# Where the matmul operands begin in a partition: moving the weight buffers and the operands that stream past them to 64 bytes past a multiple of 128

## The chip, the cores and the metric

One core of one Trainium2 chip runs the whole kernel in one launch. The metric is the device time of an execution in microseconds; lower is better. The notes below use the names of the profile: PE is TensorE's matmul, PEld its weight load, DVE is VectorE, ACT is ScalarE, POOL is GpSimd, SP issues most DMAs.

## What is computed

Two transformer blocks run one after the other on a sequence of 256 tokens with a model width of 1024. The first has a mixer of four kinds of linear attention, a cross attention to a memory of 256 rows, and a gated feed-forward part with a causal convolution of width 3. The second has two layers, each of three kinds of attention and another such feed-forward part:

```python
def reference(x, mem, positions, ...):
    x = first_block(x, mem, positions, ...)    # mixer, cross attention, conv FFN
    x = second_block(x, ...)                   # 2 x (three attentions, conv FFN)
    return x

# one feed-forward part, D_FF = 2816
    u = causal_dwconv(h @ w_up[l], conv_w[l], conv_b[l])
    gate, up = u[..., :D_FF], u[..., D_FF:]
    x = x + (jax.nn.silu(gate) * up) @ w_down[l]
```

Nearly all the arithmetic is products of an activation of 256 columns (the tokens) with weight matrices that are read once.

## The kernel before

Activations lie feature by feature: a partition holds a feature, and 256 columns of 4 bytes hold the tokens, so an operand of one product is 1024 bytes in a partition. Every number that enters a weight product is split into a high part that the fast 4-byte matmul type (float32r) holds and a low part, the rest. The weights come in 339 chunks of at most 1024 columns, in the order of use: SP loads a chunk into `raw`, ACT writes the high part `whi` and DVE the low part `wlo` (`load`, lines 396 to 414, three buffers of each). A product of 128x128 weights with 256 tokens is then three matmuls (`mm_f`, lines 422 to 431):

```python
            nc.tensor.matmul(ps, wh, xh[:, k, :], start=s, stop=False, skip_group_check=True)
            nc.tensor.matmul(ps, wh, xl[:, k, :], start=False, stop=False, skip_group_check=True)
            nc.tensor.matmul(ps, wl, xh[:, k, :], start=False, stop=e, skip_group_check=True)
```

The second argument is the stationary operand: PE loads its 128 columns. The third is the streaming operand, whose 256 columns pass through. So 128x128 weights are loaded for each matmul, and the load for the next one runs while the present one streams. In `mm_t` (lines 433 to 442), used where the result is wanted token by token, the roles are turned: the activation is stationary and the weights stream.

The stages, in order of time: the mixer (`block1_mix`, products into `psz`, `psq`, `psr`, `pst`), the keys of the memory (`psk`), the mixer's output product (`psW` from `oh`), the cross attention (`psv`, `psq`, and `po` from `xph`, whose stationary operand is the value tile `vh`), its output product (`psW` from `xoh`), and then three times a feed-forward part (`ffn`, tags f0, l0f, l1f) with a layer of attention (`attn`: `psp`, `pst`, then `psW` from `aoh`) before the second and third. A feed-forward part has 1056 matmuls up (`psU`, from `xh`, `xl`) and 528 down (`psD`, from `gh`, `gl`). A scheduler orders the instructions of each engine from the program's text and its own costs.

Tiles are given addresses by pools that stand one behind another in a partition, so an odd size moves all that follow. In `ffn` (line 627) a small tile `gpad` of 8, 16 or 72 columns (32, 64 or 288 bytes) is put ahead of `gh` and `gl`. By the built program's addresses the operands begin in a partition, in bytes past a multiple of 256:

| stationary in `mm_f` | streaming in `mm_f` | others |
|---|---|---|
| `whi`, `wlo` 128 | `xh`, `xl` 160; `gh`, `gl` 160 (f0), 192 (l0f), 160 (l1f); `mh`, `ml`, `oh`, `ol` 224; `xoh`, `xol` 0; `aoh`, `aol`, `lath` 128 | `xph` 64 streams past `vh` 224; `kh` 0 past `qh` 0 |

Blocks of 128 weights begin at multiples of 512 bytes in their buffer, and the blocks of an activation at multiples of 1024, so these differences hold for nearly all products. (Exceptions are the weights of `t0`, 280 and 264 columns wide, and four blocks behind them.)

Two masks of 128x128, `triu` and `strict`, are loaded with the constants of block 1 into `cst1` (line 747). Lines 912 and 913 copy them on DVE into the last 256 columns of `levr`, whose first 896 a DMA on POOL's queue fills (line 750).

## Time and profile before

| | us |
|---|---|
| median of three runs | 1169.15 (1167.93 to 1175.37) |
| the profiled execution, as timed | 1173.19 |
| its span in the profile | 1171.4 |

The profile shows one execution. Busy times of PE are sums of intervals in which a matmul was under way. Matmuls are pipelined: one lasts about 0.28 us in the trace while the next starts some 0.115 us after it. What counts is therefore the number of matmuls in a stretch. A row for a stretch counts each instruction that was under way in it, so two of the matmuls it counts began before it.

### The profile page before, as it was taken

The numbers are of one execution on the slowest core, as the hardware profiler recorded it, in microseconds if no ns is written. First come the engines' busy times: TensorE is split into PE (matmuls) and PEld (weight loads), VectorE is DVE, ScalarE is ACT, GpSimd is POOL, SyncE is SP. The second block draws the span as 40 slices with busy tenths as digits, with TensorE's granted clock in tenths as the row PEclk, the third lists the DMA queues.
The fourth block names the chain that finished last, engine by engine and source line by source line (L and its number), as shares of the span: only waits on it lengthen the run. The fifth ranks groups of instructions, "written<-read, shape, count | busy, mean of one in ns | idle before, by whom it ended". The sixth has DMA issues, their size and how long they took to land.

```text
span 1171.4 us, 23197 instructions
## 1 busy us (share of the span) xinstructions
PE 1141.4 (97%) x9148; PEld 1098.4 (94%) x9148; DVE 937.7 (80%) x1887; ACT 668.4 (57%) x1178; POOL 109.0 (9%) x137
## 2 busy tenths in 40 slices
PE   8999999999999999998999999999999999999996
PEld 7799888989999999997989999999998999999996
DVE  7887869586599997568997899986577978999854
ACT  6562545566476566553555676664545556766642
POOL 5500201010010000222000200001120002000000
PEclk9999999999999999998999999999999999999999
DMA  7522242556455655553423555556543235556552
GB/s 244 167 76 77 69 144 73 178 175 218 129 167 195 197 183 193 185 165 121 142 95 110 179 193 186 191 188 197 184 143 124 93 125 171 189 187 194 184 192 87
DMA packets 51948, 184.68 MB, mean 158 GB/s; under 512 B 5888, under 2 KB 6784, under 8 KB 51584
## 3 DMA queue, kind: packets, MB, share of 16 engines
q1 hardware_dynamic: 51408, 182.23, 48.1%
q8 instruction: 71, 1.16, 0.4%
q0 software_dynamic: 144, 0.46, 0.1%
q10 hardware_dynamic: 288, 0.52, 0.1%
q14 instruction: 37, 0.30, 0.1%
HBM read 182.14 MB, written 1.05 MB: 156 GB/s over the span
## 4 chain that ended last, share of the span: by engine, by line
PE 87%; DVE 9%; ACT 2%; issue 1%; DMA 0%; SPq 0%; POOL 0%; DVEq 0%; ACTq 0%
PE psU L431 10%; PE psU L429 10%; PE psU L430 10%; PE psD L429 5%; PE psD L431 5%; PE psD L430 5%; PE psp L429 3%; PE psp L430 3%; PE po L451 3%; PE psp L431 3%; PE psW L429 3%; PE psW L431 3%; PE psW L430 2%; DVE wlo L411 2%; PE pss L451 2%; PE pst L442 2%
## 5 line engine op out<-in xcount | busy, mean ns | idle before, releaser
L410 ACT ACTIVATE whi<-raw 128x1024 fp32r<-128x1024 f32 (+5 forms) x411 | 362.9, 898 | 311.8 <-PE psU L430 60.0
L411 DVE TENSOR_TENSOR wlo<-raw,whi 128x1024 fp32r<-128x1024 f32 (+5 forms) x411 | 423.9, 1043 | 135.6 <-ACT whi L410 133.1
L429 PE MATMUL psU<-xh,whi 128*128 128x256 f32 x1056 | 295.9, 280 | 0.0
L431 PE MATMUL psU<-xh,wlo 128*128 128x256 f32 x1056 | 295.4, 280 | 0.2 <-DVE wlo L411 0.2
L430 PE MATMUL psU<-xl,whi 128*128 128x256 f32 x1056 | 295.2, 280 | 0.0
L431 PEld LDWEIGHTS psU<-xh,wlo 128*128 128x128 f32 x1056 | 198.8, 188 | 0.4 <-DVE wlo L411 0.4
L429 PEld LDWEIGHTS psU<-xh,whi 128*128 128x128 f32 x1056 | 198.9, 188 | 0.1
L430 PEld LDWEIGHTS psU<-xl,whi 128*128 128x128 f32 x1056 | 198.8, 188 | 0.1
L429 PE MATMUL psD<-gh,whi 128*128 128x256 f32 x528 | 147.1, 279 | 0.0
L431 PE MATMUL psD<-gh,wlo 128*128 128x256 f32 x528 | 147.1, 279 | 0.0
L430 PE MATMUL psD<-gl,whi 128*128 128x256 f32 x528 | 147.1, 279 | 0.0
L534 POOL TENSOR_TENSOR ssa<-ssa,ssq 128x256 f32<-128x256 f32 x61 | 55.4, 912 | 721.3 <-ACT ssq L532 442.2
L666 DVE SCALAR_TENSOR_TENSOR y<-zb,prm,y 128x256 f32<-128x256 f32 x264 | 114.3, 482 | 0.0
L430 PEld LDWEIGHTS psD<-gl,whi 128*128 128x128 f32 x528 | 99.3, 188 | 0.0
L429 PEld LDWEIGHTS psD<-gh,whi 128*128 128x128 f32 x528 | 99.3, 188 | 0.0
L431 PEld LDWEIGHTS psD<-gh,wlo 128*128 128x128 f32 x528 | 99.3, 188 | 0.0
L429 PE MATMUL psp<-xh,whi 128*128 128x256 f32 (+1 forms) x288 | 85.4, 297 | 0.0
L430 PE MATMUL psp<-xl,whi 128*128 128x256 f32 (+1 forms) x288 | 84.3, 293 | 0.0
L431 PE MATMUL psp<-xh,wlo 128*128 128x256 f32 (+1 forms) x288 | 84.0, 292 | 0.0
L657 ACT ACTIVATE y<-zb,prm 128x256 f32<-128x256 f32 x132 | 67.2, 558 | 4.8 <-DVE zb L653 4.7
L442 PE MATMUL pst<-wlo,xh 128*128 128x256 f32 (+3 forms) x176 | 56.5, 321 | 1.9 <-DVE wlo L411 1.9
L429 PEld LDWEIGHTS psp<-xh,whi 128*128 128x128 f32 (+1 forms) x288 | 55.5, 193 | 3.0 <-issue 2.3
(456 smaller groups left out, 2350.2 us busy)
## 6 DMA issues: line engine op xcount, KB each, us to landing
raw<-in_wst_dram SPq DMA_DIRECT2D x319, 512.0 KB, 3.5
raw<-in_wst_dram SPq DMA_DIRECT2D x5, 448.0 KB, 3.3
cst<-in_c_dram SPq DMA_DIRECT2D x1, 1664.0 KB, 7.1
raw<-in_wst_dram SPq DMA_DIRECT2D x3, 396.0 KB, 2.9
mem<-in_memT_dram SPq DMA_DIRECT2D x1, 1024.0 KB, 5.3
raw<-in_wst_dram SPq DMA_DIRECT2D x2, 480.0 KB, 3.9
raw<-in_wst_dram SPq DMA_DIRECT2D x2, 420.0 KB, 7.2
raw<-in_wst_dram SPq DMA_DIRECT2D x2, 384.0 KB, 4.3
```

The source lines that it names most:

```text
L410: nc.scalar.activation(hi[:, a:b], raw[:, a:b], AF.Copy)
L411: nc.vector.tensor_sub(lo[:, a:b], raw[:, a:b], hi[:, a:b].bitcast(F32))
L429: nc.tensor.matmul(ps, wh, xh[:, k, :], start=s, stop=False, skip_group_check=True)
L430: nc.tensor.matmul(ps, wh, xl[:, k, :], start=False, stop=False, skip_group_check=True)
L431: nc.tensor.matmul(ps, wl, xh[:, k, :], start=False, stop=e, skip_group_check=True)
L442: nc.tensor.matmul(pss[t], xh[:, k, a], wl, start=False, stop=i == n - 1, skip_group_check=True)
L451: self.nc.tensor.matmul(out, lhsT, rhs, start=start, stop=stop, skip_group_check=True)
L534: (eng or nc.gpsimd).tensor_add(acc, acc, sq)
L657: nc.scalar.activation(y[:, e, u, :], z[:, e, 2:], AF.Identity, scale=fc[:, c + 2:c + 3], **kw)
L666: nc.vector.scalar_tensor_tensor(y[:, e, u, :], zs[u][:, e, j:j + T], fc[:, c + j:c + j + 1], y[:, e, u, :], ALU.mult, ALU.add)
```

## The change

Pads of 64 to 224 bytes are put ahead of the weight buffers and of five other groups of tiles, and `gh` and `gl` become slices of larger tiles. The two masks leave `cst1`; the DMA on POOL's queue brings them into `levr` together with the rest, and the later steps read them there. No product, load or conversion is added or taken away but the two copies of lines 912 and 913.

```diff
-GPAD = {"f0": 8, "l0f": 16, "l1f": 72}
+PAD = {"w": 16, "x": 56, "m": 16, "xo": 24, "lat": 8}
+GPAD = {"f0": 76, "l0f": 72, "l1f": 68}
...
+    def pad(self, pool, key):
+        if PAD[key]:
+            pool.tile([P, PAD[key]], F32, name="pad" + key)
...
             self.wraw = en("wraw", NRAW)
+            self.pad(en("wpad"), "w")
             self.whi = en("whi", NW)
...
+            self.pad(self.one, "x")
             self.prm1 = self.one.tile([P, _PWID1], F32, name="prm1")
...
-            big.tile([P, GPAD[tag]], F32, name="gpad")
-            gh = big.tile([P, NFF, T], F32R, name="gh")
-            gl = big.tile([P, NFF, T], F32R, name="gl")
+            gh, gl = (big.tile([P, NFF * T + P], F32R, name=n)[:, GPAD[tag]:GPAD[tag] + NFF * T].rearrange("p (k t) -> p k t", t=T)
+                      for n in ("gh", "gl"))
...
-                nc.gpsimd.dma_start(self.levr[:, 0:896], self.ap["c1"][:, _C1O["lev"][0]:])
+                nc.gpsimd.dma_start(self.levr, self.ap["c1"][:, _C1O["lev"][0]:])
...
-        tri, strict = self.c1("triu"), self.c1("strict")
         lev = self.levr
-        nc.vector.tensor_copy(lev[:, 896:1024], tri)
-        nc.vector.tensor_copy(lev[:, 1024:1152], strict)
+        tri, strict = lev[:, 896:1024].bitcast(F32), lev[:, 1024:1152].bitcast(F32)
...
+        self.pad(self.memp, "m")
         self.mh = self.memp.tile([P, KD, T], F32R, name="mh")
...
+        self.pad(m, "xo")
         oh = m.tile([P, KD, T], F32R, name="xoh")
...
+        self.pad(m, "lat")
         lh = m.tile([P, 3, T], F32R, name="lath")
```

By the built program's addresses the operands now begin as follows, and the last column is the start of the streaming operand less that of the stationary one, in bytes modulo 256, before and after (for `gh` modulo 128 the starts are 80, 64 and 48):

| products | streaming, after | stationary, after | difference before, after |
|---|---|---|---|
| `psU`, `psp`, `psz`, `psr`, `psq` <- `xh`, `xl` | 192 | 192 | 32, 0 |
| `psD` <- `gh`, `gl` in f0 | 208 | 192 | 32, 16 |
| the same in l0f | 192 | 192 | 64, 0 |
| the same in l1f | 176 | 192 | 32, 240 |
| `psW` <- `aoh`; `lath`; `kh` past `qh` | 192 | 192 | 0, 0 |
| `psW` <- `xoh` | 192 | 192 | 128, 0 |
| `psk` <- `mh`; `psW` <- `oh` | 64 | 192 | 96, 128 |
| `po` <- `xph` past `vh` | 0 | 64 | 96, 192 |
| `pst` <- `whi` past `xh` (`mm_t`) | 192 | 192 | 224, 0 |
| `psv` <- `whi` past `mh` (`mm_t`) | 192 | 64 | 160, 128 |

The order of the instructions changes only in the mixer: of some 8660 on PE about thirty lines of difference, none behind the first 350, and none of the products of the feed-forward parts. On DVE it changes around the two copies, at the end of the mixer's convolution. There DVE had, in the kernel before (`wlo` are weight conversions, `y` the convolution, `gl_p` gates):

```order
L411 TENSOR_TENSOR wlo<-raw,whi 128x512
L755 TENSOR_TENSOR z<-psz,iy 128x256
L411 TENSOR_TENSOR wlo<-raw,whi 128x512
L912 CAST levr<-cst_141 128x128
L411 TENSOR_TENSOR wlo<-raw,whi 128x512
L759 SCALAR_TENSOR_TENSOR y<-z,prm_86,y 128x256
L411 TENSOR_TENSOR wlo<-raw,whi 128x512
L759 SCALAR_TENSOR_TENSOR y<-z,prm_86,y 128x256
L859 TENSOR_SCALAR gl_p<-sm 128x8
L860 TENSOR_TENSOR gl_p<-sm,prm_86 128x8
L759 SCALAR_TENSOR_TENSOR y<-z,prm_86,y 128x256
L913 CAST levr<-cst_141 128x128
```

In the changed kernel the same place reads:

```order
L415 TENSOR_TENSOR wlo<-raw,whi 128x512
L764 SCALAR_TENSOR_TENSOR y<-z,prm_91,y 128x256
L415 TENSOR_TENSOR wlo<-raw,whi 128x512
L760 TENSOR_TENSOR z<-psz,iy 128x256
L415 TENSOR_TENSOR wlo<-raw,whi 128x512 x2
L764 SCALAR_TENSOR_TENSOR y<-z,prm_91,y 128x256
L864 TENSOR_SCALAR gl_p<-sm 128x8
L865 TENSOR_TENSOR gl_p<-sm,prm_91 128x8
L764 SCALAR_TENSOR_TENSOR y<-z,prm_91,y 128x256 x2
```

The two casts are gone, and one `z` stands a step or two later among the same conversions. On POOL's queue the place of the mask's DMA and of its readers is the same; before they were these rows:

```order
L750 DMA levr<-in_c_dram 128x896
L848 TENSOR_TENSOR sinR<-sinR,iy 128x256
L849 TENSOR_TENSOR cosR<-cosR,iy 128x256
L923 TENSOR_TENSOR G_659<-cst_141,glo 128x512
L923 TENSOR_TENSOR G_663<-cst_141,glo 128x512
```

and now they are these:

```order
L755 DMA levr<-in_c_dram 128x1152
L853 TENSOR_TENSOR sinR<-sinR,iy 128x256
L854 TENSOR_TENSOR cosR<-cosR,iy 128x256
L926 TENSOR_TENSOR G_662<-levr,glo 128x512
L926 TENSOR_TENSOR G_666<-levr,glo 128x512
```

The DMA has 256 columns more, and the products `G` read the mask from the tile that it fills.

## Rows read from the trace of the kernel before

**Rows 1.** The page: the span, busy time, clock, chain that ended last.
```profile
span 1171.4 us, 23197 instructions
...
PE 1141.4 (97%) x9148; PEld 1098.4 (94%) x9148; DVE 937.7 (80%) x1887; ACT 668.4 (57%) x1178; POOL 109.0 (9%) x137
...
PEclk9999999999999999998999999999999999999999
...
PE 87%; DVE 9%; ACT 2%; issue 1%; DMA 0%; SPq 0%; POOL 0%; DVEq 0%; ACTq 0%
```
**Rows 2.** Busy time by stretch: part of the mixer, the second block's attentions.
```profile
core 0: us, PE busy (x) PEld busy (x) DVE busy (x) ACT busy (x) POOL busy (x), PEclk, DMA share, GB/s
30.00:170.00 140.00, 135.15 (x940) 121.44 (x939) 111.86 (x278) 69.10 (x147) 24.47 (x30) 0.99 0.34 104
...
511.00:655.00 144.00, 138.78 (x1097) 130.03 (x1096) 118.93 (x340) 75.56 (x167) 11.94 (x11) 0.96 0.38 122
837.00:976.00 139.00, 135.78 (x1085) 127.80 (x1084) 111.03 (x325) 72.65 (x161) 11.50 (x11) 0.98 0.40 127
```
**Rows 3.** The same view: 100 us of psU in f0, l0f, l1f.
```profile
340.00:440.00 100.00, 100.00 (x859) 100.00 (x859) 96.34 (x154) 65.33 (x95) 0.00 (x0) 1.00 0.58 188
665.00:765.00 100.00, 100.00 (x858) 99.95 (x857) 94.69 (x150) 67.77 (x94) 0.00 (x0) 1.00 0.59 192
990.00:1090.00 100.00, 100.00 (x859) 100.00 (x859) 95.42 (x151) 66.94 (x93) 0.00 (x0) 1.00 0.58 189
```
**Rows 4.** The same view: 56 us of psD in f0, l0f, l1f.
```profile
452.00:508.00 56.00, 56.00 (x482) 56.00 (x482) 34.14 (x40) 31.61 (x44) 11.52 (x12) 1.00 0.58 189
780.00:836.00 56.00, 56.00 (x497) 56.00 (x496) 35.53 (x41) 29.63 (x40) 7.00 (x6) 1.00 0.59 195
1104.00:1160.00 56.00, 56.00 (x482) 56.00 (x481) 29.74 (x36) 26.68 (x36) 0.00 (x0) 1.00 0.49 157
```
**Rows 5.** The same view: unbroken psW from aoh, first and second layer.
```profile
641.24:649.15 7.91, 7.91 (x68) 7.91 (x67) 4.25 (x5) 2.74 (x4) 0.00 (x0) 1.00 0.41 140
962.94:971.09 8.15, 8.15 (x70) 8.15 (x69) 3.74 (x5) 2.50 (x3) 0.00 (x0) 1.00 0.41 145
```
**Rows 6.** The same view: psk and psW from oh; psW from xoh; pst of 256.
```profile
208.00:237.00 29.00, 29.00 (x244) 29.00 (x243) 14.92 (x24) 14.14 (x28) 0.00 (x0) 1.00 0.55 178
307.00:320.00 13.00, 13.00 (x112) 13.00 (x111) 5.76 (x9) 5.30 (x9) 0.00 (x0) 1.00 0.52 166
...
170.63:176.19 5.56, 5.56 (x49) 5.55 (x48) 2.59 (x4) 3.30 (x8) 0.00 (x0) 1.00 0.54 189
```
**Rows 7.** PE in order of time: first and last of ten consecutive matmuls into po.
```profile
281.10 0.28 PE L451 MATMUL po<-xpl,vh 128*128 128x256 f32 x1
...
282.18 0.28 PE L451 MATMUL po<-xpl,vh 128*128 128x256 f32 x1
```
**Rows 8.** Costliest groups of the page: counts of psU, psD, psp (one line of three).
```profile
L429 PE MATMUL psU<-xh,whi 128*128 128x256 f32 x1056 | 295.9, 280 | 0.0
...
L429 PE MATMUL psD<-gh,whi 128*128 128x256 f32 x528 | 147.1, 279 | 0.0
...
L429 PE MATMUL psp<-xh,whi 128*128 128x256 f32 (+1 forms) x288 | 85.4, 297 | 0.0
```
**Rows 9.** Tile levr and line 923: duration min/median/max in ns, first and last start.
```profile
L750 POOL DMA_DIRECT2D levr<-in_c_dram x1: 772/772/772, 39.3 to 39.3; - x1
L912 DVE CAST levr<-cst x1: 295/295/295, 39.8 to 39.8; 128x128 fp32r<-128x128 f32 x1
L913 DVE CAST levr<-cst x1: 219/219/219, 42.5 to 42.5; 128x128 fp32r<-128x128 f32 x1
...
DMA to landing us min/median/max: 6.4/6.4/6.4
...
L923 DVE TENSOR_TENSOR G<-cst,ghi x2: 684/684/685, 51.0 to 51.6; 128x512 fp32r<-128x512 f32 x2
```

More of the change, by code (lines that the diff above doesn't have):

```diff
@@ L211, in const_arrays @@
     c1["hind"] = hi2
-    c1["triu"] = (i[:, None] <= i[None, :])
-    c1["strict"] = (i[:, None] > i[None, :])
     lg = np.log(f(1) - np.exp2(f(-5) - np.arange(4, dtype=f))).astype(np.float64)
@@ L236, in const_arrays @@
     c1["decay"] = dec.reshape(P, -1)
-    c1["lev"] = np.concatenate(lev, 1)
+    c1["lev"] = np.concatenate(lev + [i[:, None] <= i[None, :], i[:, None] > i[None, :]], 1)
     c2["ident"] = np.eye(P)
@@ L707, in block1_mix @@
         self.cst1 = cp.tile([P, n2], F32, name="cst1")
-        n1 = _C1O["triu"][0]
+        n1 = _C1O["mlev"][0]
         m = self.mp = en("mix")
```

## The prediction

> **What bounds the kernel now.** I read the page first, then busy time by stretch, then PE in order of time. The page says that TensorE is the bound: PE is busy for 97% of the span and 87% of the chain that ended last is PE's, at a granted clock of 0.9 or more in all slices but one [rows 1]. So the next question is how fast PE's stream runs where nothing holds it up. In the feed-forward parts a row shows PE busy for all of its 100 us, DVE for 95 to 96, and 858 or 859 matmuls at a granted clock of 1.00, which is 2.4 GHz [rows 3]. Two of those began before the stretch, so a matmul starts every 100 / 857 = 116.7 ns.
>
> Here is what the reader should see next: the same form of matmul (128x128 weights, 256 columns, float32r), at the same clock, with PE busy throughout, has not one interval but several. I set each beside the difference d, the start of the streaming operand less that of the stationary one, modulo 256 bytes, from the addresses in the section on the kernel:
>
> - d = 32: psD in f0 and l1f, 56 / 480 = 116.7 ns [rows 4]; psU also 116.7 [rows 3].
> - d = 64: psD in l0f, 56 / 495 = 113.1 ns [rows 4]. Same code, same weights' order, only the operand's start differs.
> - d = 0: psW from aoh, 7.91 / 66 and 8.15 / 68 = 119.9 ns [rows 5].
> - d = 96: psk and psW from oh, 29 / 242 = 119.8 ns [rows 6].
> - d = 128: psW from xoh, 13 / 110 = 118.2 ns; d = 224: pst of 256 columns, 5.56 / 47 = 118.3 ns [rows 6].
>
> **Is it the difference, or the streaming start alone?** That decides the sign, because the change moves both operands. One place tells. In the cross attention xph streams from 64 (modulo 128) past vh, which starts at 96 there (d = 96). If a streaming start of 64 were what makes psD in l0f fast, these would take 113 ns. Nine intervals take 282.18 - 281.10 = 1.08 us, 120 ns each [rows 7], as the other pair with d = 96 does, with operands at 96 and 0 [rows 6]. So two pairs that differ in both starts but not in d agree, and two pairs with the same streaming start (64) and different d are 7 ns apart. I take it that the load of the next weights and the stream of the present matmul get into each other's way, and that how much depends on d.
>
> The Trainium skill speaks against this: "SBUF — State Buffer", section "SBUF: two separate sides", says that on the engines' side only the port pair shared by VectorE and GpSimd causes contention, and PE never waits on anyone. By it no start would matter and the change would cost nothing, near 1169 us. This trace disagrees with it by 7 ns a matmul between rows 4 and 5; I keep it as a rival.
>
> **The change part by part.** Nothing that PE does is added or removed; only d changes, so each term is matmuls times the step in their interval, from the d that they have to the d that they get.
>
> - psU, 3 x 1056 matmuls [rows 8], d from 32 to 0: 3168 x (119.9 - 116.7 = 3.2 ns) = 10.1 us. All on the path, PE being busy throughout [rows 3].
> - psD in l0f, 528 matmuls (a third of 3 x 528 [rows 8]), d from 64 to 0: 528 x (119.9 - 113.1 = 6.8) = 3.6 us.
> - psD in f0, 528, d from 32 to 16. No row has 16. It lies between 0 (+3.2) and 32 (nothing); I take the middle, 1.6 x 528 = 0.8 us. The far ends are 113.1 and 119.9: -1.9 to +1.7 us.
> - psD in l1f, 528, d from 32 to 240. Its neighbours are 224 (118.3) and 0 (119.9); middle 119.1, 2.4 x 528 = 1.3 us, with the same ends, -1.9 to +1.7 us.
> - psp, 3 x 288 [rows 8], of which 60 stream from lath at d = 0 before and after: 804 x 3.2 = 2.6 us. In the attention stretches PE is busy for 138.8 of 144 and 135.8 of 139 us [rows 2], but part of that is matmuls that wait for each other's results; I count four fifths, 2.1 us.
> - psz, psq and psr from xh: 144 + 288 + 96 = 528 by the loops, x 3.2 = 1.7 us; four fifths again (PE 135 of 140 us in the mixer [rows 2]), 1.4 us.
> - mm_t with 256 columns, 240 by the loops, d from 224 to 0: 1.6 x 240 = 0.4 us. The 144 with 264 or 280 columns have mixed starts before and after: nothing. With 512 columns (240) both operands change to d = 0 or 128 from 224 or 160; no row bounds it closely, I take nothing, with 240 x twice 1.6 = 0.8 us either way.
> - psk and psW from oh, 384, d from 96 to 128: -1.6 x 384 = -0.6 us. psW from xoh, 192, d from 128 to 0: 1.7 x 192 = +0.3 us. psW from aoh, 384, keeps d = 0: nothing. po from xph, 96, goes to d = 192, which no row has: between 113.1 and 120, -0.7 to 0; I take nothing.
> - The masks. Two copies of 0.295 and 0.219 us leave DVE [rows 9]. They stood in the mixer, where DVE is busy for 112 of 140 us and PE for 135 [rows 2], so PE's work hides them: nothing, with 0.5 us as the bound of the gain. The DMA on POOL's queue grows from 896 to 1152 columns. It was issued at 39.3 and landed 6.4 us later, near 45.7; the products G that now wait for it started at 51.0 [rows 9]. Stretched by 1152 / 896 it lands 8.2 us after its issue, at 47.5. That leaves 3.5 us, so nothing; if that cover were gone, DVE would stand in G with its weight conversions behind it, and PE's products of the mixer would come later by the same time, 3 us at worst.
>
> The sum is 10.1 + 3.6 + 0.8 + 1.3 + 2.1 + 1.4 + 0.4 - 0.6 + 0.3 = 19.4 us. The profiled execution took 1173.2 us (1171.4 of it span) and would take 1192.6. It stands 4 us above the median of 1169.15, which lies within the spread of the three runs, so on the median the same sum gives 1188.5 us, 1.7% slower. No other engine takes over: DVE had 4 to 5% to spare in psU [rows 3] and gets more when PE slows.
>
> **The rivals.**
> First, the streaming start alone decides, and 64 is the good one. Then psU, psp and the mixer's products go to 113.1: -3.6 x (3168 + 0.8 x 1332) = -15.2 us; aoh from 119.9, 384 x -6.8 = -2.6; psk, oh, -6.7 x 384 = -2.6; xoh, -5.1 x 192 = -1.0; f0 and l1f, at 80 and 48, between -3.8 and 0, say -1.9. That is -23.3 us, 1146. For it speaks psD in l0f, the only stream from 64 past weights at 0; against it the 120 ns of po [rows 7]. It decides from the point where a pair at 64 and 64 runs below 116.7. In that case DVE, at 95 to 96 of 100 us in psU [rows 3], would come within 2% of being the bound.
>
> Second, no start matters by itself or by d; the intervals come from something that the stages differ in, and the new kernel takes 1169 us. This is what the skill's rule above would make of it. Against it stand the three psD stretches, alike in all else and 3.6 ns apart.
>
> Third, slower by more: the writes of whi and wlo at the new start get slower too. DVE has 100 x 119.9 / 116.7 - 95.5 = 7 us of 103 to spare in psU, so it would have to lose more than 7% to be felt. Nothing in the trace shows this; with 10% psU would be 2 to 3 us longer in each 100, some 10 us over the three parts, 1199.
>
> **How the numbers follow.** Forecast 0.76; streaming start alone 0.13; no effect 0.08; still slower 0.03. The forecast's own range is 1181 to 1194: the sum less the fifths, the unknown d at their good ends and the mixer's terms (about 7 us), or with all of them at the bad end (about 4). The range of 8 in 10 leaves the first rival out and reaches down to the second: 1168 to 1195. About 1% (12 us) is what a measurement of this kernel can tell from no change. Slower by more than that is the forecast, but for the part where it comes out small, and the third rival: 0.76. Within 1%: 0.11. Faster: 0.13.
>
> **What would show it.** In the changed kernel 100 us of psU should hold about 836 matmuls (100 / 0.1199, and two) where 859 were; 56 us of psD in l0f about 469 where 497 were, and now fewer than in f0; psW from oh slightly more than before, psW from aoh the same. The mixer's end should move by 1 to 2 us at most. It is wrong if psU holds more than 870, and the rule on d falls if psD in l0f keeps its 497.

## The result and the profile after

The changed kernel takes 1187.56 us, the median of 4 executions (1183.63 to 1193.86); the kernel before, beside it on the same chip, 1169.37. The ratio is 1.0145, 95% interval 1.0113 to 1.0177: slower by 18.2 us, where 19.4 were forecast. (Ratios leave out executions more than 1.5% above the fastest of their kernel; in runs 6 and 9 below these belong to what is measured, and there I list all times as well.)

The page of the profiled execution, which took 1193.86 us, the longest of the four, has these lines in answer to [rows 1, 8]:

```profile
span 1192.1 us, 23193 instructions
...
PE 1164.1 (98%) x9148; PEld 1121.2 (94%) x9148; DVE 939.2 (79%) x1885; ACT 668.0 (56%) x1178; POOL 110.8 (9%) x137
...
PEclk9899989999999999998999999999999999999999
...
PE 89%; DVE 7%; ACT 2%; issue 1%; DMA 0%; SPq 0%; POOL 0%; DVEq 0%
...
L433 PE MATMUL psU<-xh,whi 128*128 128x256 f32 x1056 | 299.4, 284 | 0.0
...
L433 PE MATMUL psD<-gh,whi 128*128 128x256 f32 x528 | 148.2, 281 | 0.0
...
L433 PE MATMUL psp<-xh,whi 128*128 128x256 f32 (+1 forms) x288 | 86.1, 299 | 0.0
```

PE has as many instructions as before and 22.7 us more busy time; its share of the chain that ended last went from 87 to 89%. Next, busy time by stretch: 100 us of psU in f0, l0f and l1f, then 56 us of psD in each, which answer to [rows 3, 4]; then psW from aoh twice, psk with psW from oh, psW from xoh, and pst of 256 columns, which answer to [rows 5, 6].

```profile
core 0: us, PE busy (x) PEld busy (x) DVE busy (x) ACT busy (x) POOL busy (x), PEclk, DMA share, GB/s
350.00:450.00 100.00, 100.00 (x836) 100.00 (x835) 94.29 (x148) 62.76 (x92) 0.00 (x0) 1.00 0.56 185
680.00:780.00 100.00, 100.00 (x836) 100.00 (x835) 92.41 (x146) 65.27 (x90) 0.00 (x0) 1.00 0.56 185
1010.00:1110.00 100.00, 100.00 (x836) 100.00 (x835) 93.11 (x147) 65.53 (x92) 0.00 (x0) 1.00 0.56 184
461.00:517.00 56.00, 56.00 (x474) 56.00 (x474) 33.35 (x40) 31.59 (x44) 11.51 (x12) 1.00 0.58 183
792.00:848.00 56.00, 56.00 (x469) 56.00 (x468) 33.66 (x42) 29.16 (x39) 5.60 (x5) 1.00 0.54 183
1123.00:1179.00 56.00, 56.00 (x480) 56.00 (x480) 31.17 (x39) 27.34 (x37) 0.00 (x0) 1.00 0.49 160
...
650.50:658.41 7.91, 7.91 (x68) 7.91 (x67) 4.25 (x5) 2.75 (x4) 0.00 (x0) 1.00 0.44 141
979.98:988.12 8.14, 8.14 (x70) 8.14 (x69) 3.74 (x5) 2.50 (x3) 0.00 (x0) 1.00 0.45 148
214.00:243.00 29.00, 29.00 (x247) 29.00 (x246) 15.16 (x25) 14.23 (x28) 0.00 (x0) 1.00 0.54 178
312.00:325.00 13.00, 13.00 (x111) 13.00 (x110) 5.87 (x9) 5.21 (x9) 0.00 (x0) 1.00 0.48 163
176.65:182.21 5.56, 5.56 (x48) 5.56 (x47) 2.59 (x4) 3.28 (x7) 0.00 (x0) 1.00 0.57 189
```

Read with the count less two, as in the prediction: psU went from 116.7 to 100 / 834 = 119.9 ns, with 836 matmuls where 836 were forecast. psD in l0f fell from 497 matmuls to 469, to 119.9 ns, and is now the slowest of the three psD and no longer the fastest. psW from aoh, whose difference of starts d is 0 in both kernels, holds its 68 and 70. psk and psW from oh gained three matmuls (d from 96 to 128), psW from xoh lost one (d from 128 to 0), pst of 256 columns lost one (d from 224 to 0). The clock was 1.00 in all of these.

The stages start as follows (psk is the keys of the memory); a stage's gain is the change in the distance between starts. The columns "second" are a second profiled execution of the same changed kernel, taken later (run 10). The last column is the prediction's sum, each term put where its matmuls run: of psz, psq and psr 336 of 528 stand ahead of psk and 192 in the cross attention, and of the mm_t products with 256 columns most stand in the attention.

| stage | before, us | after | gain | after, second | gain | forecast |
|---|---|---|---|---|---|---|
| start to first psk | 178.9 | 185.0 | +6.1 | 178.2 | -0.7 | +0.9 |
| to first psU | 145.5 | 145.5 | 0 | 145.5 | 0 | +0.2 |
| psU, three together | 374.7 | 384.9 | +10.2 | 384.8 | +10.1 | +10.1 |
| psD f0 | 61.6 | 62.7 | +1.1 | 62.7 | +1.1 | +0.8 |
| psD l0f | 59.8 | 63.3 | +3.5 | 63.4 | +3.6 | +3.6 |
| psD l1f | 61.5 | 61.8 | +0.3 | 61.7 | +0.2 | +1.3 |
| attention, two layers | 279.1 | 278.6 | -0.5 | 278.6 | -0.5 | +2.4 |

### The profile page after: what moved, and what is told of

The parts are those of the page before. It is cut to its first block, busy times and chain, and to the rows that moved or that the text cites. A ratio compares the mean times of both kernels' runs of the same rounds, so it can differ in the third digit from the quotient of the medians.

```text
span 1192.1 us, 23193 instructions
## 1 busy us (share of the span) xinstructions
PE 1164.1 (98%) x9148; PEld 1121.2 (94%) x9148; DVE 939.2 (79%) x1885; ACT 668.0 (56%) x1178; POOL 110.8 (9%) x137
## 4 chain that ended last, share of the span: by engine, by line
PE 89%; DVE 7%; ACT 2%; issue 1%; DMA 0%; SPq 0%; POOL 0%; DVEq 0%
PE psU L435 10%; PE psU L434 10%; PE psU L433 10%; PE psD L435 5%; PE psD L433 5%; PE psD L434 5%; PE psp L433 3%; PE psp L434 3%; PE po L455 3%; PE psp L435 3%; PE psW L433 3%; PE psW L435 2%; PE psW L434 2%; PE pss L455 2%; DVE wlo L415 2%; PE pst L444 2%
## 5 line engine op out<-in xcount | busy, mean ns | idle before, releaser
L415 DVE TENSOR_TENSOR wlo<-raw,whi 128x1024 fp32r<-128x1024 f32 (+5 forms) x411 | 424.0, 1043 | 147.6 <-ACT whi L414 143.7
L433 PE MATMUL psU<-xh,whi 128*128 128x256 f32 x1056 | 299.4, 284 | 0.0
L435 PE MATMUL psU<-xh,wlo 128*128 128x256 f32 x1056 | 298.9, 283 | 0.1
L434 PE MATMUL psU<-xl,whi 128*128 128x256 f32 x1056 | 298.8, 283 | 0.0
L435 PEld LDWEIGHTS psU<-xh,wlo 128*128 128x128 f32 x1056 | 202.7, 192 | 0.3 <-DVE wlo L415 0.3
L434 PEld LDWEIGHTS psU<-xl,whi 128*128 128x128 f32 x1056 | 202.7, 192 | 0.1
L433 PEld LDWEIGHTS psU<-xh,whi 128*128 128x128 f32 x1056 | 202.7, 192 | 0.1
L444 PE MATMUL pst<-whi,xh 128*128 128x256 f32 (+3 forms) x176 | 57.2, 325 | 0.7 <-DVE z L760 0.7
```

The costliest lines, as they stand in the source:

```text
L415: nc.vector.tensor_sub(lo[:, a:b], raw[:, a:b], hi[:, a:b].bitcast(F32))
L444: nc.tensor.matmul(pss[t], xh[:, k, a], wh, start=i == 0, stop=False, skip_group_check=True)
```

## The experiments

From here on a stream is a row of matmuls of one form with no pause between them, and an interval is the mean distance between the starts of consecutive matmuls over a whole stream, taken from the trace's records. That is finer than a count in a window; the windows agree to 0.2 ns. Before: psU 116.7, psD 116.7, 113.3, 116.7. After: psU 120.0, psD 118.7, 120.0, 117.15.

The first four runs take the change apart.

**1. The weights back.** The changed kernel with its weight buffers where they were before (128); all streams stay where the change put them. That is d = 64 for psU, psp and the mixer, 80, 64 and 48 for psD.

```diff
-            self.pad(en("wpad"), "w")
             self.whi = en("whi", NW)
             self.wlo = en("wlo", NW)
+            self.pad(en("wpad"), "w")
```

> The changed kernel with its weight buffers 64 bytes lower (pad of 64 bytes behind wlo instead of ahead of whi): every streaming start stays as in the changed kernel, the weights begin at 128 modulo 256 as in the kernel before. d (streaming start less stationary start) is 64 for xh, aoh, xoh and gh in l0f, 80 and 48 for gh in f0 and l1f, 192 for mh and oh. Theory (the difference decides): psU, psD in l0f, psW from aoh and from xoh start every 113.3 ns instead of 120.0; 3168 x 6.7 = 21 us from psU, 3.5 from psD in l0f, 4 from aoh and xoh, 1 each from f0 and l1f, 3 to 7 from psp and the mixer's products: 1150 us (1145 to 1157), some 18 us below the kernel before. Rival (the streaming start alone): nothing moves, 1187 us, psU at 120.0. Rival (the new start of the weights costs the same whatever streams): psU as in the kernel before, 116.7, about 1172 us.

Measured: 1174.67 us, ratio 1.0043 (1.0025 to 1.0060). A miss of 25 us. Busy time by stretch, three of psU and then three of psD:

```profile
345.00:445.00 100.00, 100.00 (x851) 100.00 (x850) 95.70 (x149) 63.93 (x95) 0.00 (x0) 1.00 0.60 190
675.00:775.00 100.00, 100.00 (x851) 100.00 (x851) 93.17 (x146) 65.32 (x91) 0.00 (x0) 1.00 0.60 191
1000.00:1100.00 100.00, 100.00 (x851) 100.00 (x851) 93.82 (x147) 64.73 (x90) 0.00 (x0) 1.00 0.60 189
450.00:506.00 56.00, 56.00 (x469) 56.00 (x468) 32.92 (x39) 31.39 (x44) 11.31 (x12) 1.00 0.58 181
779.00:835.00 56.00, 56.00 (x477) 56.00 (x477) 34.38 (x40) 28.91 (x39) 7.00 (x6) 1.00 0.60 188
1103.00:1159.00 56.00, 56.00 (x475) 56.00 (x474) 30.63 (x38) 27.11 (x36) 0.00 (x0) 1.00 0.49 158
```

At d = 64 psU runs at 117.8 ns, not at 113.3. Most telling is the fifth row: psD in l0f has the same two starts as in the kernel before, where 497 matmuls fitted into 56 us [rows 4], and here it has 477. So the two starts alone do not fix the interval.

**2. Everything moved by 32 bytes.** The kernel before, masks kept once, and 32 bytes ahead of the weights, which push all that follows: both starts of nearly all operands move, and no d does. (The masks' part of the edit is left out below.)

```diff
+            en("wpad").tile([P, 8], F32, name="padw")
             self.whi = en("whi", NW)
```

> The kernel before with the masks kept once (room for the rest) and 32 bytes put ahead of the weight buffers, so that the starts of nearly all operands move by 32 bytes and every d stays as in the kernel before: weights at 160 modulo 256, xh at 192 (64 modulo 128). Theory (the difference decides): all intervals as before: psU 116.7, psD 116.7, 113.3, 116.7 ns in f0, l0f, l1f, psW from aoh 120; time as the kernel before, 1169 us within 3. Rival (streaming and stationary start each have a cost of their own, which add up): with the costs of the streaming starts read off the kernel before (0: 119.9, 32: 116.7, 64: 113.2, 96: 119.8), psD in l0f (now at 96) becomes slower than psU and psD in f0 and l1f (now at 64) by 6.6 ns, and psW from aoh (now at 32) faster than it by 3; the order of the three psD stretches turns round.

Measured: 1170.93 us, ratio 0.9988 (0.9965 to 1.0011). psU in f0, then psD in f0 and in l0f, to be set beside [rows 3, 4]:

```profile
340.00:440.00 100.00, 100.00 (x859) 100.00 (x859) 96.51 (x153) 64.92 (x95) 0.00 (x0) 1.00 0.61 189
452.00:508.00 56.00, 56.00 (x482) 56.00 (x482) 32.62 (x37) 31.66 (x44) 11.53 (x12) 1.00 0.61 188
780.00:836.00 56.00, 56.00 (x496) 56.00 (x495) 34.32 (x39) 28.56 (x38) 7.99 (x7) 1.00 0.62 196
```

With both operands moved alike nothing changes, to one matmul. So a shift by 32 bytes that leaves d as it is does not count.

**3. The masks alone.** The kernel before with the two masks kept once, and no start moved.

```diff
-    c1["triu"] = (i[:, None] <= i[None, :])
-    c1["strict"] = (i[:, None] > i[None, :])
...
-        nc.vector.tensor_copy(lev[:, 896:1024], tri)
-        nc.vector.tensor_copy(lev[:, 1024:1152], strict)
```

> The kernel before with only the masks' part of the change: two copies fewer on DVE, the DMA on the POOL queue 256 columns longer, every start that matters as before. Theory: nothing, 1169 us within 2; the first psk, which began 6.1 us later in the changed kernel's profile than in that of the kernel before, begins as before (179 us, within 2). Rival: the masks account for most of those 6.1 us, in the mixer: 1173 us or more.

Measured: 1171.51 us, ratio 1.0020 (1.0007 to 1.0034); its first psk starts at 178.1 us where 178.9 stood before. By the 95% interval that is 0.8 to 4.0 us slower; run 2, which keeps the masks once as well, shows no cost. Either way it is not the 18.

**4. The weights further.** The changed kernel with weights at 0 in place of 192 and all streams unmoved, so d goes to 192, that is -64, for psU and 208, 192 and 176 for psD.

```diff
-PAD = {"w": 16, "x": 56, "m": 16, "xo": 24, "lat": 8}
+PAD = {"w": 32, "x": 40, "m": 16, "xo": 24, "lat": 8}
```

> The changed kernel with its weight buffers 64 bytes higher (pad ahead of whi 128 bytes, the next pad 64 bytes smaller): streaming starts unchanged, weights at 0 modulo 256, d = 192 for xh, aoh, xoh and gh in l0f, 64 for mh and oh, 208 and 176 for gh in f0 and l1f. Theory with a period of 128 bytes: as e1, psU at 113.3, 1150 us (1145 to 1157). Theory with a period of 256 bytes, and d = 192 as po from xph has it in the changed kernel (117.6 ns over 40 intervals): psU at 117.6, 1187 - 3168 x 2.4 - 3 = 1176 us (1171 to 1181). Rival (the streaming start alone): 1187 us.

Measured: 1175.96 us, ratio 1.0058 (1.0041 to 1.0075). (The pad of lat in these lines is 32 bytes, so the change's pads go from 32 to 224 bytes, ahead of the weights and of four other groups.) The time is what a period of 256 bytes was said to give, but not for its reason: psU runs at 117.8 ns in all three parts, as at d = 64, while many shorter streams at d = 192 (psp, psW from aoh) run at 113.3. So at d = 64 and at d = 192 two steady intervals exist, 113.3 and 117.8 ns. In the records nearly every stream takes one of them within some six matmuls and holds it to its end, over 1559 matmuls in the longest case. (These are not the only values of d with two. In the kernel before, at d = 32, the 90 products of psU ahead of psS in l1f run at 117.8 ns, as they do in runs 2, 3 and 5, and so do several psp streams of 20 to 48; the long parts of psU run at 116.7. At d = 128 psk and psW from oh run at 118.6 ns in the changed kernel, but one psk stream of 55 at 120.0.) psU behind the float32 products psS, where its second start comes 305 ns after its first, took 117.8 six times of six in runs 1 and 4; psD of l0f in the kernel before follows psU at d = 32 without a gap and takes 113.3.

That gave a second theory: the two starts set which intervals are possible, and what ran just ahead of the stream (its entry) picks one. The next four runs test it, and the part of the change that was left.

**5. psD at d = 64 in all three parts.** The kernel before but for the pads ahead of gh and gl.

```diff
-GPAD = {"f0": 8, "l0f": 16, "l1f": 72}
+GPAD = {"f0": 16, "l0f": 16, "l1f": 16}
```

> The kernel before, with the pads in front of gh and gl made equal, so that the down products of all three FFNs run at d = 64, as those of l0f already do; the up products stay at d = 32. Theory (the stream that a product follows on picks which of the two intervals of d = 64 it takes; after the unbroken up products at d = 32 that is 113.3 ns): psD of f0 and l1f go from 116.7 to 113.3 ns, 2 x 528 x 3.4 ns = 3.6 us less, about 1165.4 us. Rival (the value at d = 64 is drawn anew, or belongs to the weights of l0f alone): 117.8 ns in f0 and l1f, 2 x 528 x 1.1 ns = 1.2 us more, about 1170 us.

Measured: 1168.87 us beside 1172.1 for the kernel before, ratio 0.9977 (0.9956 to 0.9999). psD in f0, l0f and l1f:

```profile
450.00:506.00 56.00, 56.00 (x497) 56.00 (x496) 34.72 (x41) 32.37 (x46) 11.57 (x12) 1.00 0.57 194
776.00:832.00 56.00, 56.00 (x497) 56.00 (x496) 35.54 (x43) 30.52 (x40) 7.00 (x6) 1.00 0.58 191
1099.00:1155.00 56.00, 56.00 (x496) 56.00 (x496) 31.78 (x39) 28.32 (x39) 0.00 (x0) 1.00 0.51 166
```

All three hold 496 or 497 where f0 and l1f held 482 [rows 4]: 113.3 ns, as the theory has it. The ratio makes that 2.7 us (0.1 to 5.2), where 3.6 were expected.

**6 and 7. A lead at d = 32, and one at d = 64.** Run 1 with gh at d = 64 everywhere; ahead of the first up product behind psS stand 12 products of the same form whose result is thrown away.

```diff
-GPAD = {"f0": 76, "l0f": 72, "l1f": 68}
+GPAD = {"f0": 72, "l0f": 72, "l1f": 72}
...
+                        if i + u == FIRST:
+                            for _ in range(12):
+                                nc.tensor.matmul(p2[:, 0, :], self.w(f"{tag}g{FIRST}", 0)[0], xh.rearrange("p k t -> p (k t)")[:, 248:504], start=True, stop=True, skip_group_check=True)
```

Columns 248 to 504 give d = 32; run 7 has 256 to 512, d = 64.

> The first experiment (weights back at 128, streams at 192, d = 64) with gh at d = 64 in all three FFNs, and, in front of the first up product behind the psS products in each FFN, 12 more products of 256 columns at d = 32 whose result is thrown away. Theory (the entry picks the interval): after the lead at d = 32 the up products run at 113.3 ns in place of 117.8, 3 x 960 x 4.45 ns = 12.8 us less than the first experiment, and the down products follow them, 528 x (6.7 + 4.5 + 5.0) ns = 8.6 us less; the leads cost 3 x 12 x 0.117 = 4.2 us: 1174.7 + 4.2 - 21.4 = about 1157.5 us. Rival (the up products take 117.8 ns at these starts whatever comes before): about 1177 us.

> As the run with the lead at d = 32, but the 12 thrown-away products of each FFN begin at d = 64 like those behind them. Theory: the lead itself enters the 117.8 ns interval behind the psS products and the up and down products hold it: 1174.7 + 4.2 - 528 x (2.2 + 0.6) ns = about 1177.4 us. Rival (12 more products of any kind at the front are enough): 113.3 ns, about 1157.5 us.

Measured: run 7 1180.16 us (1179.01 to 1183.34), ratio 1.0088 (1.0058 to 1.0118). Run 6 has a median of 1168.86, ratio 0.9973 (0.9947 to 1.0000), where 1157.5 us were expected, and its ten executions lie far apart: 1159.3, 1164.2, 1164.2, 1166.0, 1167.0, 1170.8, 1172.0, 1172.0, 1173.0 and 1178.8. The profiled one is the fastest, and it alone comes near the expectation. Its psU in three parts, and psD in l0f:

```profile
345.00:445.00 100.00, 100.00 (x885) 100.00 (x884) 97.08 (x153) 66.54 (x96) 0.00 (x0) 1.00 0.61 196
665.00:765.00 100.00, 100.00 (x884) 100.00 (x884) 95.91 (x150) 68.17 (x93) 0.00 (x0) 1.00 0.59 195
985.00:1085.00 100.00, 100.00 (x885) 100.00 (x884) 95.82 (x150) 68.18 (x95) 0.00 (x0) 1.00 0.59 194
...
770.00:826.00 56.00, 56.00 (x497) 56.00 (x496) 35.62 (x42) 30.11 (x40) 7.03 (x6) 1.00 0.59 193
```

And of run 7 the same:

```profile
345.00:445.00 100.00, 100.00 (x852) 100.00 (x851) 95.20 (x148) 62.57 (x92) 0.00 (x0) 1.00 0.57 190
675.00:775.00 100.00, 100.00 (x851) 100.00 (x851) 92.70 (x144) 65.05 (x90) 0.00 (x0) 1.00 0.56 186
1000.00:1100.00 100.00, 100.00 (x851) 100.00 (x850) 93.01 (x145) 65.02 (x90) 0.00 (x0) 1.00 0.57 188
...
783.00:839.00 56.00, 56.00 (x478) 56.00 (x478) 34.69 (x41) 29.20 (x39) 6.41 (x6) 1.00 0.57 189
```

From the first up product behind the lead on the two kernels issue the same matmuls with the same operands at the same starts, at the same clock, and one runs at 113.3 ns, the other at 117.8, for up to 1560 matmuls on end. The only difference is what 12 thrown-away products ahead of them streamed. So in these two executions the entry picked the interval, in three parts of three each. The spread of run 6 fits it too: a part of 960 up and 528 down products that misses 113.3 costs 1488 x 4.45 = 6.6 us, and the times stand near 1159 plus none, one, two or three times that. Only the profiled execution can be looked into, so for the others this is argued.

**8. The weights alone.** The weights 64 bytes on, as in the change; all streams where they were before.

```diff
-PAD = {"w": 16, "x": 56, "m": 16, "xo": 24, "lat": 8}
-GPAD = {"f0": 76, "l0f": 72, "l1f": 68}
+PAD = {"w": 16, "x": 48, "m": 0, "xo": 0, "lat": 0}
+GPAD = {"f0": 8, "l0f": 16, "l1f": 72}
```

> The weights alone moved 64 bytes on, every stream left at its start of before (masks kept once). Theory (only the difference of the starts counts): psU at d = 224, 118.3 ns (3168 x 1.6 = 5.1 us more), psD of l0f at d = 0, 120 ns (528 x 6.7 = 3.5 more), psD of f0 and l1f 1.7 more, psp and the mixer's products 1 to 1.5 more, aoh at d = 192 from 119.8 to 113.4 or 117.8 (0.8 to 2.5 less), oh and mh at d = 32 1.2 less: about 1177.5 us, some half of what the whole change adds. Rival (the place of the weights in the partition by itself costs the change's 18 us): about 1187 us; or (only the streams' start counts): 1169 us.

Measured: 1178.56 us, ratio 1.0075 (1.0049 to 1.0101). psU in f0, then psD in f0 and l0f:

```profile
340.00:440.00 100.00, 100.00 (x848) 100.00 (x847) 95.53 (x150) 64.35 (x94) 0.00 (x0) 1.00 0.56 185
...
451.00:507.00 56.00, 56.00 (x476) 56.00 (x475) 33.45 (x41) 31.68 (x44) 11.54 (x12) 1.00 0.57 183
779.00:835.00 56.00, 56.00 (x469) 56.00 (x468) 33.72 (x41) 29.11 (x39) 5.59 (x5) 1.00 0.57 185
```

118.3, 118.3 and 120.0 ns, each as the prediction's list has it for d = 224 and d = 0, from quite other places in the kernel. With runs 1 and 8 the change falls into parts: the streams alone cost 0.4%, the weights alone 0.75%, both together 1.45%. The parts need not add up to the whole, since each sets other differences d.

The last four runs ask how the entry picks, and settle the mixer.

**9. Leads of other lengths.** Run 6 with 10, 11 and 13 products in place of 12 (f0, l0f, l1f).

```diff
-                            for _ in range(12):
+                            for _ in range({"f0": 10, "l0f": 11, "l1f": 13}[tag]):
```

> As the run with 12 leading products at d = 32, but 10 of them in f0, 11 in l0f and 13 in l1f. In the profiled execution of that run the intervals of each lead went 117 118 118 116 117 120 114 115 118 120 113, the last one to the first up product at d = 64, so the three lengths change over at the 118, the 120 and the 116 of the pattern of four. Theory A (the place in the pattern at which the start changes picks the interval, and the other executions of that run, 1159 to 1179 us in steps of some 6 us, missed it in none to three FFNs): at least one of the three FFNs runs its up and down products at 117.8 ns, 6.6 us each: 1166 to 1179 us, with the FFNs that miss it in the profile longer by that much. Theory B (any lead at d = 32 enters 113.3): all three at 113.3, the profiled execution about 1159 us.

Measured: median 1172.78 us beside 1168.27, ratio 0.9991 (0.9950 to 1.0033); the ten executions took 1157.7, 1168.2, 1171.3, 1172.4, 1172.4, 1173.1, 1175.4, 1175.7, 1176.8 and 1177.6. In the profiled execution, of 1176.75 us, all three parts of psU run at 117.8 ns:

```profile
345.00:445.00 100.00, 100.00 (x851) 100.00 (x850) 95.04 (x148) 62.53 (x92) 0.00 (x0) 1.00 0.59 190
670.00:770.00 100.00, 100.00 (x851) 100.00 (x851) 92.84 (x145) 65.13 (x91) 0.00 (x0) 1.00 0.56 186
1000.00:1100.00 100.00, 100.00 (x851) 100.00 (x850) 92.48 (x144) 64.46 (x90) 0.00 (x0) 1.00 0.59 188
```

The intervals of the leads go in a pattern of four, about 113 116 117 120 (116.7 on average). In runs 5 and 6, six parts, the change of start came behind the 113 (or 114), and all six took 113.3; so did psD of l0f in the kernel before and in runs 2 and 3. Here it came behind 118, 120 and 120, and all three took 117.8. That is in keeping with theory A, that the place in the pattern at which the start changes decides, in all twelve parts. (A lead can also run in another pattern, 117 117 116, of the same mean; the one lead seen in it, in l1f of the probe below, led to 117.8.)

**10. The changed kernel once more.** Unaltered.

> The changed kernel unaltered, for a second profiled execution. In the first one the first product of the mixer's second half began 6.1 us later than before, where 1.8 were forecast, at a lower granted clock up to 180 us, and that execution was the longest of its runs. Theory (the rest is that execution's clock): the same start lies 1 to 3 us later than before (180 to 182 us) when the clock is as before, and the span is about 1185 us. Rival (the moved starts delay the mixer by 6 us): 185 us again.

Measured: 1186.72 us (1183.02 to 1187.11), ratio 1.0137 (1.0094 to 1.0180). Its first psk starts at 178.2 us. From 140 to 180 us the first changed execution, and then this one:

```profile
140.00:180.00 40.00, 39.51 (x220) 35.42 (x218) 24.52 (x71) 17.36 (x35) 0.00 (x0) 0.87 0.38 120
```

```profile
140.00:180.00 40.00, 39.45 (x244) 34.38 (x243) 26.96 (x75) 20.12 (x40) 0.00 (x0) 1.00 0.46 144
```

At a mean granted clock of 0.87 instead of 1.00 (2.4 GHz), PE gets through 220 matmuls instead of 244. The same kernel reached its first psk 6.8 us apart in two executions, so the 6.1 us belonged to that execution and its clock, not to the change; every other stage repeats to 0.1 us in the table above.

**11. A probe.** Run 6, with rows of 20 thrown-away products at d = 64 behind each lead, and between the rows 1 to 8 products at d = 32 (f0, behind a lead of 10, and l0f, behind 12), or 1 to 4 at other starts (l1f).

```diff
+                            seq = [(32, 10 if tag == "f0" else 12)]
+                            ins = [(32, n) for n in (1, 2, 3, 4, 5, 6, 7, 8)] * 2 if tag != "l1f" else [(d, n) for d in (0, 16, 48, 96, 128, 192, 224) for n in (1, 2, 3, 4)]
+                            for q in ins:
+                                seq += [(64, 20), q]
+                            for d, n in seq + [(64, 20)]:
+                                o = 240 + d // 4
...
```

> A measurement, not a candidate: as the run with 12 leading products, but each lead is followed by rows of 20 thrown-away products at d = 64 with 1 to 8 products at another start set in between (d = 32 in f0, behind a lead of 10, and in l0f, behind a lead of 12; d = 0, 16, 48, 96, 128, 192 and 224, 1 to 4 of each, in l1f); some 172 us longer. Theory (the interval at d = 64 is a state that a change of the start can set and can lose): some of the inserts turn rows of 117.8 ns into rows of 113.3 ns and the other way, and which do so goes by their number and start, not by chance. Rival 1 (a state once taken holds until the engine waits): f0 stays at 117.8 and l0f and l1f at 113.3 throughout. Rival 2 (every insert draws anew): about one row in two at 113.3 whatever the insert.

One execution, 1337.31 us. What the row of 20 behind each insert did, worked out from the start times in the trace (f0 and l0f, each insert four times):

```
inserted at d = 32   row before -> row behind (ns), times
1 product            117.8 -> 113.3, 1     113.3 -> 117.8, 3
2                    117.8 -> 117.8, 3     113.3 -> 117.8, 1
3                    117.8 -> 113.3, 4
4                                          113.3 -> 113.3, 4
5                                          113.3 -> 117.8, 4
6                    117.8 -> 113.3, 4
7                                          113.3 -> 117.8, 4
8                    117.8 -> 113.3, 4
```

Both rivals fall: a few products at another start move the stream from one interval to the other with no pause between, and for 3 to 8 of them the outcome was the same each time. The leads fit theory A again: f0's ended behind a 117 and led to 117.8, l0f's behind a 113 and led to 113.3. At the other starts only 16 (4 products), 96 (4) and 224 (2) led from 117.8 to 113.3; 21 further inserts left 117.8 as it was. The up products behind the probe kept what its last row had, 113.3 in f0 and l0f and 117.8 in l1f.

**12. Three products between.** Run 6 without its lead; behind the first tile that follows psS, and ahead of the next, three thrown-away products at d = 32.

```diff
-                        if i + u == FIRST:
-                            for _ in range(12):
+                        if i + u == FIRST + 1:
+                            for _ in range(3):
```

> A version that the probe points to: the weights at 128, all streams of the up and down products at d = 64 as in the run with the lead, but no lead; behind the 48 products of the first tile that follows the psS products stand 3 thrown-away products at d = 32. Theory (behind the psS products the stream enters 117.8 ns; three products at d = 32 brought it from there to 113.3 in four cases of four; from there it holds through the down products): up products 113.3 ns from the second tile on, down products 113.3 ns, in nearly every execution: 1174.7 - 3 x 912 x 4.45 ns - 528 x 11.5 ns for the down products (20 us less than the first experiment and 1 us for the thrown-away ones) = about 1157 us, and a spread no wider than that of the kernel before. Rival (what the probe showed holds for its one repeated weight tile alone, or only in a profiled execution): 1165 to 1177 us, in steps of some 6 us.

Measured: 1165.67 us, ratio 0.9965 (0.9938 to 0.9992), twelve executions from 1159.83 to 1174.97. It beats both kernels, but the one before by 0.35%, not by the 1% expected. (The 11.5 ns in the expectation should have been 16.2, which makes the forecast 2.5 us lower still.) psU in the profiled execution, of 1159.87 us:

```profile
345.00:444.00 99.00, 99.00 (x876) 99.00 (x876) 96.52 (x153) 64.94 (x95) 0.00 (x0) 1.00 0.63 195
670.00:769.00 99.00, 99.00 (x843) 99.00 (x843) 91.84 (x144) 63.61 (x89) 0.00 (x0) 1.00 0.59 191
988.00:1087.00 99.00, 99.00 (x876) 99.00 (x875) 95.46 (x150) 68.51 (x96) 0.00 (x0) 1.00 0.59 192
```

f0 and l1f reach 113.3, l0f stays at 117.8. The three intervals of the insert were 116 120 120, 116 116 115 and 117 120 120; in the probe, where three always worked, they were 116 or 117 120 120 three times and 114 121 113 once, and never 116 116 115. So two streams that both show 117.8 seem to stand in different places of a pattern that this interval hides, and an insert of fixed length meets only some of them; no run tests this. The rival was right about the time: 1165 us and more, where about 1157 were expected.

## Why the prediction was right, and where its reasons were not

*The total.* Forecast 1188.5, measured 1187.56. Some 15 of the 18 us lie where the prediction put most of the cost: in the intervals of psU and psD at a clock of 1.00, with DVE not the bound (92 to 94 of 100 us in psU after).

*psU, 10.1 us.* Measured 10.2 and 10.1. The 119.9 ns for d = 0 came from psW into another tile and held.

*psD, l0f, 3.6 us.* Measured 3.5 and 3.6. This was the sign that the rule on d would fall by, and it passed.

*psD in f0 and l1f, 0.8 and 1.3 us.* Measured 1.1 and 0.2 to 0.3. Estimated between neighbours, as no row had these starts: f0 118.7 ns for 118.3 assumed, l1f 117.15 for 119.1. So l1f's term was mis-sized by 1.0 us. The interval is no smooth curve in d: 224 and 0 have 118.3 and 120.0, and 240 between them 117.15.

*psp and the mm_t products of the attention, 2.4 us.* Smaller than that, as far as the clock lets it be told. The attention stretches of the two layers went from 141.8 to 140.6 us and from 137.3 to 138.0; the kernel before and after:

```profile
511.10:652.90 141.80, 136.58 (x1078) 127.83 (x1077) 116.83 (x336) 73.46 (x162) 11.20 (x10) 0.96 0.39 123
837.10:974.40 137.30, 134.08 (x1070) 126.10 (x1069) 109.43 (x321) 71.06 (x158) 10.06 (x9) 0.98 0.40 127
```

```profile
521.60:662.20 140.60, 135.54 (x1079) 126.92 (x1078) 116.99 (x336) 73.51 (x163) 11.22 (x10) 0.98 0.38 124
853.40:991.40 138.00, 134.92 (x1070) 127.10 (x1069) 109.47 (x321) 70.97 (x158) 10.07 (x9) 0.98 0.40 126
```

In the second layer, at one clock, the gain is 0.7 us where half of 2.4 was forecast. In the first the clock was 0.96 before and 0.98 after, which outweighs it. Runs 3 and 2, with every d as before, show how far the same code moves from one execution to the next, at other clocks: the first layer in run 3, the second in run 2.

```profile
510.00:648.90 138.90, 133.64 (x1079) 125.39 (x1078) 116.79 (x336) 73.50 (x163) 11.21 (x10) 0.99 0.40 126
834.10:968.20 134.10, 130.86 (x1070) 123.12 (x1069) 109.22 (x321) 71.19 (x158) 10.06 (x9) 1.00 0.42 130
```

Each is some 3 us shorter than in the profile of the kernel before, more than the whole term. At 0.98 run 2 has 140.3 us in the first layer, where the changed kernel has 140.6, so at a like clock the two layers gained about 1.0 us. One reason stands in the records: several psp streams already ran at 117.8 ns, the other interval of d = 32, so that their step to 120.0 was 2.2 ns and not 3.2.

*The mixer's products and mm_t there, 0.9 us.* The first execution gave +6.1 and run 10 -0.7, at other clocks, so the term can't be told. A term that the prediction put at nothing, mm_t with 512 columns, went the other way: inside their streams the 144 of pst, all in the mixer, start every 228.6 and 228.3 ns in the two executions after (d = 0) and every 233.3 before (d = 224), which is 0.7 us less. It is inside the 0.8 us that the prediction gave it, but with 512 columns d = 0 is the faster of the two.

*The masks, nothing.* Not quite settled: run 2 shows no cost, and run 3 one of 0.8 to 4.0 us, but its first psk is not late (178.1 us). What the prediction feared did not come: the longer DMA landed after 6.2 us, not 6.4 or the 8.2 that I had stretched it to, and the products G started at 51.3 us where 51.0 stood before [rows 9].

*Why the total came out so near.* In part by luck. The 18.2 us are known to 13.2 to 20.7 by their interval. The profiled execution of the kernel before was timed at 1173.19, 4 us above its median, and 3.0 of them lie in the first attention, at its clock of 0.96. Run 3 makes the better pair: its profiled execution, 1169.13, lies near the median of the kernel before, and run 10's, 1186.99, near that of the changed one. Of the 17.9 us between these two, psU and psD give 15.1, where 15.8 were forecast, and the two attentions 2.5 (1.8 and 0.7), part of it clock (0.99 against 0.98 in the first layer). So psU and psD, at a clock of 1.00, came out 0.7 us below their forecast, and the rest was not measured apart from the clock.

*The rivals.* "The streaming start alone decides" (1146) fell at once, and in run 8 psU went to 118.3 ns with every stream left in its place. "No start matters" (1169) fell. The Trainium skill's "SBUF — State Buffer", section "SBUF: two separate sides", by which PE never waits on anyone, was taken by the prediction to mean that no start matters. That does not hold here: with the starts moved, psU went from 116.7 to 120.0 ns at a clock of 1.00. Whether PE waits on anyone in this no run shows. The third rival, slower writes of whi and wlo, fell too: the page has 1043 ns on average for a conversion into wlo before and after, and 898 and 897 for one into whi.

*The reason itself.* The prediction took it that the difference of the starts sets the interval. That is half of it. It held where the records show one steady interval (d = 0 gave 120.0 in psU, psD and psW alike, d = 224 gave 118.3 in psU, psD and pst). It failed at d = 64, where the prediction had a single stretch and read its 113.1 ns as the price of d; it was the price of d after an unbroken stream at d = 32. The forecast hardly leaned on the failed half, since the change moves psD of l0f away from d = 64 to a value with one interval. That too was luck: nothing in the prediction weighed it. Run 1, which leaned on it, missed by 25 us.

## What to carry to other kernels

Where PE is the bound and weights are loaded for every matmul, set the intervals of unbroken streams of one form beside each other at the same clock, with the starts of both operands in a partition: a few per cent can lie between them, and a pad of some bytes moves it. Judge a pad by a run, not by a rule read from one stretch: the same pair of starts gave 113.3 or 117.8 ns here, by what ran just ahead. And look at the spread of executions, since a stream that may enter either interval can make times in steps, as in run 6.

## What the runs showed of the hardware that was not expected

Two steady intervals for one pair of starts, 113.3 and 117.8 ns at d = 64, held for as long as the stream is unbroken (1560 matmuls), and changed from one to the other by as few as one product at another start (probe). No unbroken stream of matmuls of 256 columns had a steady interval below 113.3 ns.

A weight load also takes longer at d = 0: in psU 192 ns on average after, 188 before. The groups of the page, after and then before:

```profile
L435 PEld LDWEIGHTS psU<-xh,wlo 128*128 128x128 f32 x1056 | 202.7, 192 | 0.3 <-DVE wlo L415 0.3
```

```profile
L431 PEld LDWEIGHTS psU<-xh,wlo 128*128 128x128 f32 x1056 | 198.8, 188 | 0.4 <-DVE wlo L411 0.4
```

In run 8, psD of l0f at d = 0 has 192.0 as well, and psD of f0 at d = 224 has 188.4. But the two intervals of d = 64 do not differ in it: 187.7 ns in run 6, 187.6 in run 7. That the load of the next weights and the present stream get into each other's way in reading may lie behind all of this, but no run took the load away or moved it in time, so that cause is argued and not shown.
